# State-space chunks stored by place in a block, gate products held back during the scan, rotation split into additions and a background rest

## The chip, the cores and the metric

The kernel runs on one core of one Trainium2 chip, in one launch. The metric is the device time of that launch in microseconds (us), as a median of runs. A profile of one execution gives, engine by engine, what each instruction did. The engines are PE (matrix multiply, with its weight loads shown apart as PEld), DVE (vector), ACT (scalar: copies, activations), POOL and SP; here SP issues nearly all DMA transfers, one after the other from one queue.

## The reference, cut to what matters

One decoder layer on 512 tokens of width 2048, in float32:

```python
h = rmsnorm(x, g_mix) * (1 + sc1) + sh1
u, q, k, v = jnp.split(h @ w_in, ...)
y_ssm = s5_mixer(u, ...)                       # diagonal complex state space, then gelu and a gate
y_att = dilated_attention(q, k, v, positions)  # q and k rotated (rope), three dilated branches
y = jnp.concatenate([rmsnorm(y_ssm), rmsnorm(y_att)], axis=-1)
x = x + gt1 * (y @ w_out)
h = rmsnorm(x) * (1 + sc2) + sh2
x = x + gt2 * ((silu(h @ w_gate) * (h @ w_up)) @ w_down)
```

The six vectors sh1, sc1, gt1, sh2, sc2, gt2 are `silu(c) @ w_mod + b_mod`: one vector times a matrix of 2048 by 12288, called gate products below. The mixer's recurrence over tokens is s[t] = a * s[t-1] + b u[t] for 64 groups of 64 complex states. Rotation is t1 * cos - t2 * sin and t2 * cos + t1 * sin on the two halves of a head.

## The kernel before, in words

Each large matrix product is done in three passes (`mm3`, L191 to L193): a float32 weight is split into a rounded part `hi` (ACT, L161) and a rest `lo` (DVE, L165), and so is the activation. A product of 512 output rows takes weight pieces of two 128-row blocks; a piece is 24 matmuls on PE (4 row groups, 2 blocks, 3 passes), with three buffers for the split pieces and five for the raw ones that SP loads (L153). Results go to four banks `g` in the accumulator memory (PSUM), and the next product's first matmul into a bank waits until that bank is read.

Beside the products run generators (`start`, `pump`): before each 128-row block of a product, `pump` advances every background generator by its rate. A scheduler then sets the order on each engine, which may put an instruction ahead of one that the code wrote earlier; the order rows below show what it made.

The stage around the change begins with `win3`. Four products of w_in finish q and k (blocks 0, 2, 1, 3 of 512 rows, with 12, 10, 12 and 10 row blocks left to do). After each, `rope(b)` rotates the four results: `r0` loads the partial sum stored earlier (L900, from `part`), adds the bank to it (L901, this frees the bank) and has ACT copy the two halves crosswise (L903); `r1` does two products and a sum on DVE (L908 to L910) and stores (L912). Before the change `r0` of one result and `r1` of the result before it alternate, all at the end of the product, in a pool `rt` of four tiles.

Beside them runs `s5_main` at rate 1. The 512 tokens are 64 chunks j of T = 8 tokens; u is stored and loaded by chunk. PE makes the chunks' inputs (L790), ACT copies them to the state tile X (L797), [128 partitions, real and imaginary, 32 groups, 1 + 64 chunks]. The scan on DVE sees the 64 chunks as 8 blocks b of 8 places i, j = 8 b + i. For i = 1 to 7 four instructions of 512 elements handle all 8 blocks at once (L814, L815, L817, L818); so neighbouring elements of X lie 8 floats, 32 bytes, apart. Then seven steps over the blocks' ends (L823 to L825, 128 and 64 elements), then eight pairs that add each block's start to its inner places (L835, L837, 784 elements). Then, for eight parts of eight groups, the output phase: ACT copies states to `sst` (L845), SP loads tables `mt` (L852) and `qt` (L861), PE multiplies (L866, L867), ACT applies gelu (L874), PE transposes (L883), ACT writes the result back in token order (L886). The first `mt` shares its buffer with the scan's last temporary, so it loads only when the scan is over.

The generator `mod_blocks(GT1)` runs at rate 0.28 from `win3`: each step loads 512 KB of w_mod (L305, three buffers `mraw`) and multiplies on DVE (L314). After `win4` (products with w_glu, which need the whole output of the state space) `mod_blocks(SC2, SH2)` runs as well, beside the attention; both take the next piece from one list of 160, the last of which the feed-forward stage needs.

Of the kernel before, what the change touches and what calls it, by code (L numbers as in the profile page):

```python
# [10 lines left out]
F32 = mybir.dt.float32  # L11
# [3 lines left out]
ALU = mybir.AluOpType  # L15

P = 128
S = 512
# [9 lines left out]
EPS = 1e-6  # L28
T = 8
NJ = S // T  # L30
SCALE = 128 ** -0.5

V_BMOD, V_GMIX, V_GFFN, V_GFIN, V_BGLU, V_GSSM, V_GATT, V_C = 0, 96, 112, 128, 144, 152, 160, 168
# [12 lines left out]
def hybrid_block(ctx: ExitStack, tc: tile.TileContext, xT, crow, vecs, pos, kc, km, w_mod, w_in, s5a, s5bc,  # L46
# [279 lines left out]
    def mod_blocks(*bases, after=None):  # L326
        for b in bases:
# [6 lines left out]
            if b == SC2:  # L334
                modulate(gs2, SC2, V_GFFN)

    def sumsq(acc, x, first):
# [250 lines left out]
    def u_store(pss):  # L588

        for m, ps in enumerate(pss):  # L590
            t = st()
            ACT.copy(t.rearrange("p (s j) -> p s j", s=T), ps.rearrange("p (j s) -> p s j", s=T))
            SP.dma_start(ud[m * P:(m + 1) * P], t)

    gemm(wiv, UC, 0, range(KT), act_h, u_store, w=2 * S)
# [176 lines left out]
    def s5_main():  # L772
        with tc.tile_pool(name="s5m", bufs=1, side="right", reuse_waits="tile") as sp, \
                tc.tile_pool(name="s5n", bufs=2, side="right", reuse_waits="tile") as sq:
            X = sp.tile([P, 2, NG // 2, NJ + 1], F32, name="s5X")
            DVE.memset(X[:, :, :, 0:1], 0.0)
            st_ = {}
            Ug = U[0]


            def u2(c):
                st_[c] = dict(pm=[vg[:, (2 * c + i) % 8].rearrange("p (g x) -> p g x", g=4) for i in range(2)])
                for i, pm in enumerate(st_[c]["pm"]):
                    SP.dma_start(pm, Pd[2 * c + i].rearrange("p (g x) -> p g x", g=4))

            def u3(c):
                d = st_[c]
                d["pi"] = mps()
                for i in range(8):
                    PE.matmul(d["pi"][:, i * NJ:(i + 1) * NJ], d["pm"][i // 4][:, i % 4], Ug[:, 8 * c + i], start=True,  # L790
                              stop=True)

            def u4(c):
                pv = st_.pop(c)["pi"].rearrange("p (g h j) -> p g h j", h=2, j=NJ)
                for h in range(2):
                    for r in range(2):
                        ACT.copy(X[64 * h:64 * h + 64, r, 4 * c:4 * c + 4, 1:], pv[64 * r:64 * r + 64, :, h])  # L797

            yield from pipe(range(8), u2, skip, u3, u4)
            yield  # L800

            NB = NJ // 8
            Xv = X[:, :, :, 1:].rearrange("p r g (b i) -> p r g b i", i=8)

            def bb(a):
                return a.unsqueeze(3).to_broadcast([P, 2, NP, NB])

            def rgb(tag):
                return sq.tile([P, 4, P], F32, tag="tA", name=nm(tag)).rearrange(
                    "p a b -> p (a b)").rearrange("p (r g b) -> p r g b", r=2, g=NP)  # L810

            for i in range(1, 8):
                t0, t1 = rgb("t0"), rgb("t1")
                tt(t0, Xv[:, :, :, :, i - 1], bb(A8[:, 0]), op=ALU.mult)  # L814
                tt(t1, Xv[:, :, :, :, i - 1], bb(A8[:, 1]), op=ALU.mult)  # L815
                yield
                tt(Xv[:, :, :, :, i], Xv[:, :, :, :, i], t0, op=ALU.add)  # L817
                tt(Xv[:, :, :, :, i], Xv[:, :, :, :, i], t1[:, ::-1], op=ALU.add)  # L818
                yield
            tmp = sp.tile([P, 2, 2, NP], F32, name="s5t")  # L820
            for b in range(1, NB):
                xn = Xv[:, :, :, b, 7]
                tt(tmp, Xv[:, :, :, b - 1, 7].unsqueeze(1).to_broadcast([P, 2, 2, NP]), A64, op=ALU.mult)  # L823
                tt(xn, xn, tmp[:, 0], op=ALU.add)
                tt(xn, xn, tmp[:, 1, ::-1], op=ALU.add)  # L825
                if b % 3 == 0:
                    yield
            for h in range(2):
                pr = slice(16 * h, 16 * h + 16)
                for o, r, p_, op in ((0, 0, 0, ALU.add), (0, 1, 1, ALU.subtract), (1, 1, 0, ALU.add),  # L830
                                     (1, 0, 1, ALU.add)):
                    t = sp.tile([P, T, P], F32, tag="tB", name=nm("tc")).rearrange("p a b -> p (a b)")
                    t = t[:, :16 * 49].rearrange("p (g b i) -> p g b i", g=16, b=7)
                    xo = Xv[:, o, pr, 1:, 0:7]
                    tt(t, Xv[:, r, pr, 0:7, 7].unsqueeze(3).to_broadcast([P, 16, 7, 7]),  # L835
                       PW[:, p_, pr, 0:7].unsqueeze(2).to_broadcast([P, 16, 7, 7]), op=ALU.mult)
                    tt(xo, xo, t, op=op)  # L837
                    yield

            def y0(c):  # L840
                prs = slice(4 * c, 4 * c + 4)
                sst = sq.tile([P, 8, NJ], F32, tag="tC", name=nm("sst")).rearrange("p (a b) j -> p a b j", b=2)
                for h in range(2):
                    for r in range(2):
                        ACT.copy(sst[64 * r:64 * r + 64, :, h], X[64 * h:64 * h + 64, r, prs, 0:NJ])  # L845
                st_[c] = dict(sst=sst)

            def y0b(c):
                mt = vg[:, (0, 4, 6)[i]:][:, :2].rearrange("p a (b x) -> p (a b) x", x=P) if (
                    i := (0, 1, 2, 0, 1, 2, 0, 2)[c]) else sp.tile([P, T, P], F32, tag="tB", name=nm("mt"))  # L850
                kc0 = Kd[:, c * P:(c + 1) * P]
                SP.dma_start(mt, bass.AP(tensor=kc0.tensor, offset=kc0.offset,  # L852
                                         ap=[[WS, P], [GC * WS, T], [1, P]]))
                st_[c]["mt"] = mt

            def y1(c):
                d = st_[c]
                d["ps"] = []
                for hh_ in range(2):
                    qt = sq.tile([P, 4, P], F32, tag="tA", name=nm("qt"))  # L860
                    SP.dma_start(qt, Qd[2 * c + hh_].rearrange("p (g x) -> p g x", g=4))  # L861
                    ps = mps()
                    for i in range(4):
                        g = 4 * hh_ + i
                        o = ps[0:NJ, i * P:(i + 1) * P]
                        PE.matmul(o, Ug[:, 8 * c + g], d["mt"][:, :, g * GC:(g + 1) * GC], start=True, stop=False)  # L866
                        PE.matmul(o, d["sst"][:, g // 2, g % 2], qt[:, i], start=False, stop=True)  # L867
                    d["ps"].append(ps)

            def y2(c):  # L870
                d = st_[c]
                d["yv"] = yv = sp.tile([NJ, T, P], F32, tag="ug", name=nm("yv"))
                for hh_, ps in enumerate(d["ps"]):
                    ACT.activation(  # L874
                        yv[:, :, hh_ * 64:hh_ * 64 + 64].rearrange("p t (g c) -> p g t c", g=4),
                        ps[0:NJ].rearrange("p (g t c) -> p g t c", g=4, t=T), AF.Gelu_apprx_tanh)

            def y3(c):
                d = st_[c]
                d["pt"] = mps()  # L880
                for t_ in range(T):
                    sl = T - 1 - t_
                    PE.transpose(d["pt"][:, sl * NJ:(sl + 1) * NJ], d["yv"][:, t_], ident[:NJ, :NJ])  # L883

            def y4(c):
                ACT.copy(vg[:, c].rearrange("p (j s) -> p s j", s=T),  # L886
                         st_.pop(c)["pt"].rearrange("p (s j) -> p s j", s=T))

            yield from pipe(range(8), y0, y0b, y1, y2, y3, y4)

# [2 lines left out]
    def rope(b):  # L893

        def f(pss):
            ts = {}

            def r0(m):
                ts[m] = pt, sw = [rst.tile([P, S], F32, tag="rt", name=nm("rt")) for _ in range(2)]
                SP.dma_start(pt, part[4 * b + m])  # L900
                tt(pt, pss[m], pt, op=ALU.add)  # L901
                for h in (0, 64):
                    ACT.copy(sw[64 - h:128 - h], pt[h:h + 64])  # L903
# [666 lines left out]
```

## Time and profile before

| what | before |
|---|---|
| runs, us | 2193.1, 2188.76, 2193.03 |
| median, us | 2193.03 |
| the profiled execution's own time, us | 2189.05 |
| its span, us | 2187.2 |
| mean granted TensorE clock | 0.984 |
| PE / DVE / ACT busy, share of the span | 96% / 69% / 39% |

The span is what the profile shows between the first and the last instruction; the own time is what was measured for that same execution. A share of busy time is a mean over stages with different limits, so a stage has to be looked at in its own stretch of time. Around this change the landmarks are, in us from the span's start: first scan instruction 352.6, last one 464.2, first output matmul of the state space 470.2, last output copy 519.4.

### The profile page before, as it was taken

The page shows a single profiled execution, that of the slowest core. Times are in us where ns is not written, and L with a number is a line of the kernel's source. Part 1 is how long each engine was busy: PE and PEld are TensorE (multiplying, and loading weights), DVE is VectorE, ACT ScalarE, POOL GpSimd, SP SyncE. Part 2 cuts the span into 40 slices and gives each one's busy share as a digit, 9 for nine tenths or more (in the row PEclk, how much of TensorE's full clock was granted, in tenths as well). Part 3 has the DMA queues.
Part 4 walks back from the last instruction along what each step waited for, and adds up shares of the span by engine and source line. Part 5 has one row for each costly group of instructions (what it writes and reads, how often), then busy time and mean ns, then how long its engine had stood idle before and what let it go on. Part 6 is the DMA issues. An engine that isn't in the chain of part 4 may idle for free.

```text
span 2187.2 us, 32392 instructions
## 1 busy us (share of the span) xinstructions
PE 2109.8 (96%) x12800; PEld 1874.8 (86%) x12800; DVE 1516.8 (69%) x2216; ACT 849.6 (39%) x1209; POOL 2.0 (0%) x7
## 2 busy tenths in 40 slices
PE   6999999889999999999999999999999999999996
PEld 4778787767787778999999999999999888888885
DVE  7896886986888776687887888878887543242224
ACT  3432343257753253444444444444444111121111
POOL 0000000000000000000000000000000000000000
PEclk9999988999999999999999999999999999999998
DMA  9999785768887633343343333434435999655552
GB/s 344 339 357 174 215 248 197 238 210 296 299 284 249 219 114 97 130 144 123 135 138 132 128 135 131 143 123 136 138 132 217 323 320 327 204 195 194 193 173 77
DMA packets 212047, 435.92 MB, mean 199 GB/s; under 512 B 50676, under 2 KB 87924, under 8 KB 211896
## 3 DMA queue, kind: packets, MB, share of 16 engines
q1 hardware_dynamic: 211656, 433.13, 59.8%
q8 instruction: 101, 1.65, 0.3%
q0 software_dynamic: 240, 0.72, 0.1%
q14 instruction: 50, 0.41, 0.1%
HBM read 380.38 MB, written 53.41 MB: 198 GB/s over the span
## 4 chain that ended last, share of the span: by engine, by line
PE 73%; DVE 8%; DMA 3%; issue 1%; ACT 0%; DVEq 0%; SPq 0%; ACTq 0%
PE g L191 11%; PE g L193 11%; PE g L192 11%; PE y L1436 5%; PE y L1437 5%; PE y L1438 5%; PE z L1437 3%; PE x L1437 3%; PE x L1436 3%; PE z L1436 3%; PE x L1438 3%; PE z L1438 3%; DMA mraw<-in_w_mod 3%; DVE mraw L314 1%; DVE lo L165 1%
## 5 line engine op out<-in xcount | busy, mean ns | idle before, releaser
L165 DVE TENSOR_TENSOR lo<-raw,hi 128x1024 fp32r<-128x1024 f32 x192 | 234.2, 1221 | 323.8 <-ACT hi L161 323.7
L161 ACT CAST hi<-raw 128x1024 fp32r<-128x1024 f32 x192 | 201.6, 1052 | 557.4 <-PE g L192 356.3
L1167 ACT CAST hi<-raw 128x1024 fp32r<-128x1024 f32 x176 | 185.1, 1052 | 292.5 <-PE x L1437 125.4
L314 DVE SCALAR_TENSOR_TENSOR mraw<-mraw,cb 128x1024 f32<-128x1024 f32 x192 | 232.1, 1219 | 75.8 <-DMA mraw<-in_w_mod 75.6
L1169 DVE TENSOR_TENSOR lo<-raw,hi 128x1024 fp32r<-128x1024 f32 x176 | 215.1, 1223 | 90.2 <-ACT hi L1167 90.1
L191 PE MATMUL g<-f,hi 128*128 128x512 f32 x704 | 273.9, 389 | 0.0
L192 PE MATMUL g<-f,hi 128*128 128x512 f32 x704 | 273.9, 389 | 0.0
L193 PE MATMUL g<-f,lo 128*128 128x512 f32 x704 | 273.9, 389 | 0.0
L1167 ACT CAST hi<-s 128x1024 fp32r<-128x1024 f32 x120 | 126.3, 1053 | 165.0 <-PE y L1437 82.8
L1436 PE MATMUL y<-t,hi 128*128 128x256 f32 x640 | 179.8, 281 | 0.0
L1437 PE MATMUL y<-t,hi 128*128 128x256 f32 x640 | 179.8, 281 | 0.0
L1438 PE MATMUL y<-t,lo 128*128 128x256 f32 x640 | 179.8, 281 | 0.0
L1437 PE MATMUL x<-b,hi 128*128 128x256 f32 x640 | 179.8, 281 | 0.0
L1436 PE MATMUL x<-b,hi 128*128 128x256 f32 x640 | 179.8, 281 | 0.0
L1438 PE MATMUL x<-b,lo 128*128 128x256 f32 x640 | 179.8, 281 | 0.0
L1169 DVE TENSOR_TENSOR lo<-s,hi 128x1024 fp32r<-128x1024 f32 x120 | 146.5, 1221 | 16.3 <-ACT hi L1167 15.7
L193 PEld LDWEIGHTS g<-f,lo 128*128 128x128 f32 x704 | 132.1, 188 | 27.5
L191 PEld LDWEIGHTS g<-f,hi 128*128 128x128 f32 x704 | 132.1, 188 | 27.4
L192 PEld LDWEIGHTS g<-f,hi 128*128 128x128 f32 x704 | 132.1, 188 | 27.3
L191 PE MATMUL g<-hB,hi 128*128 128x512 f32 x288 | 115.6, 403 | 12.8 <-DVE rt L901 12.8
L1436 PEld LDWEIGHTS x<-b,hi 128*128 128x128 f32 x640 | 120.6, 188 | 0.0
L1437 PEld LDWEIGHTS x<-b,hi 128*128 128x128 f32 x640 | 120.6, 188 | 0.0
(321 smaller groups left out, 4935.4 us busy)
## 6 DMA issues: line engine op xcount, KB each, us to landing
mraw<-in_w_mod SPq DMA_DIRECT2D x192, 512.0 KB, 6.0
raw<-in_w_down SPq DMA_DIRECT2D x88, 512.0 KB, 3.9
f<-fd SPq DMA_DIRECT2D x88, 512.0 KB, 4.2
raw<-in_w_gate SPq DMA_DIRECT2D x80, 512.0 KB, 3.3
raw<-in_w_up SPq DMA_DIRECT2D x80, 512.0 KB, 3.8
raw<-in_w_in SPq DMA_DIRECT2D x64, 512.0 KB, 5.2
fd<-fo SPq DMA_DIRECT2D x40, 512.0 KB, 4.5
raw<-in_w_out SPq DMA_DIRECT2D x32, 512.0 KB, 5.4
```

The lines of the kernel that those rows point to most:

```text
L161: ACT.copy(hi, p["raw"])
L165: tt(p["hl"][1], p["raw"], p["hl"][0].bitcast(F32), op=ALU.subtract)
L191: PE.matmul(ps, lhs[0], rhs[0], start=first, stop=False)
L192: PE.matmul(ps, lhs[0], rhs[1], start=False, stop=False)
L193: PE.matmul(ps, lhs[1], rhs[0], start=False, stop=last)
L314: stt(raw, raw, 1.0, cb[:, h * (D // 2):(h + 1) * (D // 2)], op0=ALU.mult, op1=ALU.mult, accum_out=macc[:, m, h:h + 1])
L1167: ACT.copy(hi, raw)
L1169: tt(lo, raw, hi.bitcast(F32), op=ALU.subtract)
L1436: PE.matmul(o, hi[:, sl], bh[:, k], start=f, stop=False, skip_group_check=True)
L1437: PE.matmul(o, hi[:, sl], bo[:, k], start=False, stop=False, skip_group_check=True)
L1438: PE.matmul(o, lo[:, sl], bh[:, k], start=False, stop=l, skip_group_check=True)
```

## The change

1. Chunks are stored by place in a block, then by block: j' = 8 i + b. `u_store` writes u in that order (ACT now reads the bank with a step of 64 floats along b), X gets 8 columns ahead of the 64 instead of one, and the scan's eight elements of one place lie side by side. One DVE copy is new: it puts the seven block ends into columns 1 to 7, so that columns 0 to 63 are again "the state before each chunk". The last output copy (L886 before, L898 after) writes tokens in order from the new chunk order, with a step of 64 floats where it was 8.
2. `away` wraps `mod_blocks(GT1)`: the generator takes no step while 'scan' is in `made`, which is set from the scan's first to its last step; its rate becomes 0.45.
3. `rope`: the four `r0` come first, in one go; the four `r1` become a generator at rate 1. The partial sum now lies in the staging pool (`st`, five tiles, shared with other copies), and only the crosswise copy in `rt`.

```diff
-            X = sp.tile([P, 2, NG // 2, NJ + 1], F32, name="s5X")
+            NB = NJ // NI
+            X = sp.tile([P, 2, NG // 2, NB + NJ], F32, name="s5X")
...
-            Xv = X[:, :, :, 1:].rearrange("p r g (b i) -> p r g b i", i=8)
+            made.add('scan')
+            Xv = X[:, :, :, NB:].rearrange("p r g (i b) -> p r g i b", i=NI)
...
-                tt(t0, Xv[:, :, :, :, i - 1], bb(A8[:, 0]), op=ALU.mult)
+                tt(t0, Xv[:, :, :, i - 1], bb(A8[:, 0]), op=ALU.mult)
...
+            DVE.tensor_copy(X[:, :, :, 1:NB], Xv[:, :, :, 7, 0:7])
...
+            made.remove('scan')
...
-            ACT.copy(t.rearrange("p (s j) -> p s j", s=T), ps.rearrange("p (j s) -> p s j", s=T))
+            ACT.copy(t.rearrange("p (s i b) -> p s i b", s=T, i=NI), ps.rearrange("p (b i s) -> p s i b", s=T, i=NI))
...
-                ts[m] = pt, sw = [rst.tile([P, S], F32, tag="rt", name=nm("rt")) for _ in range(2)]
+                ts[m] = pt, sw = st(), rst.tile([P, S], F32, tag="rt", name=nm("rt"))
...
-            for _ in pipe(range(4), r0, r1):
-                pass
+            def rest():
+                for m in range(4):
+                    r1(m)
+                    yield
+            for m in range(4):
+                r0(m)
+            hh.append(start(rest(), 1))
...
-        hg.append(start(mod_blocks(GT1), 0.28))
+        hg.append(start(away(mod_blocks(GT1), 'scan'), 0.45))
```

The first rotation on DVE (the end of the first of the four products) stood so before; `g_2725` to `g_2728` are the four banks, `lo_` the next weight pieces:

```order
L901 TENSOR_TENSOR rt_3028<-g_2725,rt_3028 128x512
L165 TENSOR_TENSOR lo_3069<-raw_2757,hi_3068 128x1024
L818 TENSOR_TENSOR s5X<-s5X,t_3115 128x64x8
L908 TENSOR_TENSOR rt_3028<-rt_3028,cosT 128x512
L909 TENSOR_TENSOR rt_3029<-rt_3029,sinT 128x512
L814 TENSOR_TENSOR t_3153<-s5X,A_248 128x512
L910 TENSOR_TENSOR rt_3028<-rt_3028,rt_3029 128x512
L901 TENSOR_TENSOR rt_3038<-g_2726,rt_3038 128x512
```

And so now, where L913 is the addition and L920 to L922 the rest:

```order
L913 TENSOR_TENSOR st_3034<-g_2725,st_3034 128x512
L828 TENSOR_TENSOR s5X<-s5X,t_3065 128x64x8
L315 SCALAR_TENSOR_TENSOR mraw_2958,macc<-mraw_2958,cb 128x1024
L913 TENSOR_TENSOR st_3040<-g_2726,st_3040 128x512
L920 TENSOR_TENSOR st_3034<-st_3034,cosT 128x512
L913 TENSOR_TENSOR st_3046<-g_2727,st_3046 128x512
L913 TENSOR_TENSOR st_3052<-g_2728,st_3052 128x512
```

Between the first two additions stood six instructions, now two; the fourth followed 21 instructions after the first, now six. In later products the four additions stand in one run, or one scan step apart.

The steps over the block ends (L823 to L825 before, L833 to L835 now) stand on DVE like this before:

```order
L823 TENSOR_TENSOR s5t<-s5X,A_249 128x128
L165 TENSOR_TENSOR lo_3472<-raw_3226,hi_3471 128x1024
L824 TENSOR_TENSOR s5X<-s5X,s5t 128x64
L314 SCALAR_TENSOR_TENSOR mraw_3599,macc<-mraw_3599,cb 128x1024
L825 TENSOR_TENSOR s5X<-s5X,s5t 128x64
L314 SCALAR_TENSOR_TENSOR mraw_3737,macc<-mraw_3737,cb 128x1024
```

and like this now:

```order
L833 TENSOR_TENSOR s5t<-s5X,A_249 128x128
L315 SCALAR_TENSOR_TENSOR mraw_3912,macc<-mraw_3912,cb 128x1024
L834 TENSOR_TENSOR s5X<-s5X,s5t 128x64
L315 SCALAR_TENSOR_TENSOR mraw_4156,macc<-mraw_4156,cb 128x1024
L835 TENSOR_TENSOR s5X<-s5X,s5t 128x64
L315 SCALAR_TENSOR_TENSOR mraw_4167,macc<-mraw_4167,cb 128x1024
```

So gate products still stand inside the scan, since the scheduler moves them up to where it sees DVE idle. From the scan's first to its last instruction DVE has 15 weight splits, 13 gate products and 48 rotation instructions before, and 14, 9 and 45 now, beside the scan's own 28, 21 and 16 (and the new copy).

On PE the last inputs of the chunks (L790 before, L800 now) stand before the scan; before, both of the last two parts in one go:

```order
L193 MATMUL g_2728<-hB_100,lo_2813 128x512
L790 MATMUL m_2945<-s5U,vg 128x64 x8
L790 MATMUL m_2958<-s5U,vg 128x64 x8
L191 MATMUL g_2725<-hB_100,hi_2872 128x512
L192 MATMUL g_2725<-hB_101,hi_2872 128x512
```

and now the last of them in two halves, inside the next weight piece (`lo_2876`):

```order
L192 MATMUL g_2727<-hB_100,hi_2875 128x512
L800 MATMUL m_2964<-s5U,vg 128x64 x4
L193 MATMUL g_2727<-hB_101,hi_2875 128x512
L194 MATMUL g_2727<-hB_100,lo_2876 128x512
L800 MATMUL m_2964<-s5U,vg 128x64 x4
L192 MATMUL g_2727<-hB_100,hi_2875 128x512
```

Counted from the first L790, 39 of the product's matmuls stand ahead of the last L790 before, and 54 ahead of the last L800 now. Ahead of the first output matmul of the state space (L866 before, L878 now) stand 462 of 471 such matmuls before, and 453 now. Up to the first of the attention's score readings (L1047) DVE has done 94 gate products before and 91 now.

More of the change, by code (lines that the diff above doesn't have):

```diff
@@ L30 @@
 NJ = S // T
+NI = 8
 SCALE = 128 ** -0.5
@@ L335, in mod_blocks, with away @@
                 modulate(gs2, SC2, V_GFFN)
+    def away(gen, mark):
+        for _ in gen:
+            yield
+            while mark in made:
+                yield
     def sumsq(acc, x, first):
@@ L796, in u4 @@
                     for r in range(2):
-                        ACT.copy(X[64 * h:64 * h + 64, r, 4 * c:4 * c + 4, 1:], pv[64 * r:64 * r + 64, :, h])
+                        ACT.copy(X[64 * h:64 * h + 64, r, 4 * c:4 * c + 4, NB:], pv[64 * r:64 * r + 64, :, h])
             yield from pipe(range(8), u2, skip, u3, u4)
             yield
-            NB = NJ // 8
-            Xv = X[:, :, :, 1:].rearrange("p r g (b i) -> p r g b i", i=8)
+            made.add('scan')
+            Xv = X[:, :, :, NB:].rearrange("p r g (i b) -> p r g i b", i=NI)
             def bb(a):
@@ L810, in rgb @@
                     "p a b -> p (a b)").rearrange("p (r g b) -> p r g b", r=2, g=NP)
-            for i in range(1, 8):
+            for i in range(1, NI):
                 t0, t1 = rgb("t0"), rgb("t1")
-                tt(t0, Xv[:, :, :, :, i - 1], bb(A8[:, 0]), op=ALU.mult)
-                tt(t1, Xv[:, :, :, :, i - 1], bb(A8[:, 1]), op=ALU.mult)
+                tt(t0, Xv[:, :, :, i - 1], bb(A8[:, 0]), op=ALU.mult)
+                tt(t1, Xv[:, :, :, i - 1], bb(A8[:, 1]), op=ALU.mult)
                 yield
-                tt(Xv[:, :, :, :, i], Xv[:, :, :, :, i], t0, op=ALU.add)
-                tt(Xv[:, :, :, :, i], Xv[:, :, :, :, i], t1[:, ::-1], op=ALU.add)
+                tt(Xv[:, :, :, i], Xv[:, :, :, i], t0, op=ALU.add)
+                tt(Xv[:, :, :, i], Xv[:, :, :, i], t1[:, ::-1], op=ALU.add)
                 yield
@@ L821, in s5_main @@
             for b in range(1, NB):
-                xn = Xv[:, :, :, b, 7]
-                tt(tmp, Xv[:, :, :, b - 1, 7].unsqueeze(1).to_broadcast([P, 2, 2, NP]), A64, op=ALU.mult)
+                xn = Xv[:, :, :, 7, b]
+                tt(tmp, Xv[:, :, :, 7, b - 1].unsqueeze(1).to_broadcast([P, 2, 2, NP]), A64, op=ALU.mult)
                 tt(xn, xn, tmp[:, 0], op=ALU.add)
@@ L832, in s5_main @@
                     t = sp.tile([P, T, P], F32, tag="tB", name=nm("tc")).rearrange("p a b -> p (a b)")
[L833 to L836, printed above, removed]
+                    t = t[:, :16 * 49].rearrange("p (g i b) -> p g i b", g=16, b=7)
+                    xo = Xv[:, o, pr, 0:7, 1:]
+                    tt(t, Xv[:, r, pr, 7, 0:7].unsqueeze(2).to_broadcast([P, 16, 7, 7]),
+                       PW[:, p_, pr, 0:7].unsqueeze(3).to_broadcast([P, 16, 7, 7]), op=ALU.mult)
                     tt(xo, xo, t, op=op)
                     yield
+            made.remove('scan')
             def y0(c):
@@ L885, in y4 @@
             def y4(c):
-                ACT.copy(vg[:, c].rearrange("p (j s) -> p s j", s=T),
-                         st_.pop(c)["pt"].rearrange("p (s j) -> p s j", s=T))
+                ACT.copy(vg[:, c].rearrange("p (b i s) -> p s i b", s=T, i=NI),
+                         st_.pop(c)["pt"].rearrange("p (s i b) -> p s i b", s=T, i=NI))
             yield from pipe(range(8), y0, y0b, y1, y2, y3, y4)
@@ L912, in r1 @@
                 SP.dma_start((qd if i < 8 else kd)[(i % 8) * P:(i % 8 + 1) * P], pt)
-            for _ in pipe(range(4), r0, r1):
-                pass
+            def rest():
+                for m in range(4):
+                    r1(m)
+                    yield
+            for m in range(4):
+                r0(m)
+            hh.append(start(rest(), 1))
         return f
```

## Prediction

> **What bounds the kernel now.** I read the page first, then the table by stretches of time around the scan, then waits, groups and timeline of that stretch. The page's busy rows and its chain of waits say that PE sets the time almost everywhere:
>
> ```profile
> PE   6999999889999999999999999999999999999996
> DVE  7896886986888776687887888878887543242224
> ...
> PE 73%; DVE 8%; DMA 3%; issue 1%; ACT 0%; DVEq 0%; SPq 0%; ACTq 0%
> ```
>
> Each digit is 54.7 us. DVE holds 8% of the chain, and it is the only engine beside PE that holds much. Where it does, the table by stretches shows (busy us of PE, PEld, DVE, ACT, POOL; then granted clock, DMA share, GB/s):
>
> ```profile
> 352.00:464.00 112.00, 98.34 (x401) 77.23 (x400) 109.75 (x154) 35.55 (x50) 0.00 (x0) 0.95 0.65 216
> 464.00:518.00 54.00, 49.59 (x366) 40.48 (x364) 29.25 (x45) 37.49 (x65) 0.56 (x1) 1.00 0.88 283
> 518.00:562.00 44.00, 43.90 (x204) 35.80 (x205) 35.83 (x75) 32.57 (x53) 0.00 (x0) 1.00 0.85 279
> ```
>
> The first row is the scan with three of the four rotations: DVE works 109.75 of 112 us, PE idles 112 - 98.3 = 13.7 us and runs at 0.95 of its clock (5% of 112 = 5.6 us). In the next two rows DVE has 24.8 and 8.2 us free and PE is full again. PE's waits in this stretch are for DVE:
>
> ```profile
> PE g L191 <- DVE rt L901: 12.8, 8, 3.0
> PE g L193 <- DVE lo L165: 0.9, 2, 0.6
> ```
>
> 12.8 us in eight waits go to the addition that frees a bank, which stands in DVE's queue behind scan steps, gate products and the other rotations' work. One such wait on PE's timeline, and the matmul after it, beside the one before it:
>
> ```profile
> 364.43 0.39 PE L191 MATMUL g<-hB,hi 128*128 128x512 f32 x1
> 367.79 0.79 PE L191 MATMUL g<-hB,hi 128*128 128x512 f32 x1 [2.97 <-DVE rt L901]
> 368.38 0.63 PE L192 MATMUL g<-hB,hi 128*128 128x512 f32 x1
> 368.81 0.63 PE L193 MATMUL g<-hB,lo 128*128 128x512 f32 x1
> ```
>
> After 2.97 us of idling the matmuls start 0.43 us apart; undisturbed ones do so every 0.227 us:
>
> ```profile
> 463.49 0.39 PE L191 MATMUL g<-hB,hi 128*128 128x512 f32 x1
> 463.71 0.39 PE L192 MATMUL g<-hB,hi 128*128 128x512 f32 x1
> ...
> 468.25 0.39 PE L193 MATMUL g<-hB,lo 128*128 128x512 f32 x1
> 470.22 0.41 PE L866 MATMUL m<-mt,s5U 128*64 128x128 f32 x2 [1.59 <-DMA mt<-Kd]
> ```
>
> (21 steps from 463.49 to 468.25.) The last line is the scan's end as PE sees it, 1.59 us more of waiting. So the scan's end sets when the output phase starts, and PE can win at most 13.7 + 5.6 + 1.6 = 20.9 us here.
>
> **The change part by part.** DVE's work from the scan's first to its last instruction, by groups:
>
> ```profile
> L165 DVE TENSOR_TENSOR lo<-raw,hi 128x1024 fp32r<-128x1024 f32 x16 | 19.3, 1209 | 0.0
> L314 DVE SCALAR_TENSOR_TENSOR mraw<-mraw,cb 128x1024 f32<-128x1024 f32 x13 | 15.7, 1208 | 1.4 <-DMA mraw<-in_w_mod 1.4
> L818 DVE TENSOR_TENSOR s5X<-s5X,t 128x512 f32<-128x512 f32 x7 | 8.2, 1177 | 0.0
> L901 DVE TENSOR_TENSOR rt<-g,rt 128x512 f32<-128x512 f32 x12 | 8.1, 678 | 0.0
> ...
> L817 DVE TENSOR_TENSOR s5X<-s5X,t 128x512 f32<-128x512 f32 x7 | 8.1, 1155 | 0.0
> L814 DVE TENSOR_TENSOR t<-s5X,A 128x512 f32<-128x512 f32 x7 | 7.9, 1135 | 1.9 <-ACT s5X L797 1.8
> L815 DVE TENSOR_TENSOR t<-s5X,A 128x512 f32<-128x512 f32 x7 | 7.8, 1109 | 0.0
> L837 DVE TENSOR_TENSOR s5X<-s5X,tc 128x784 f32<-128x784 f32 x8 | 7.7, 966 | 0.0
> ...
> L824 DVE TENSOR_TENSOR s5X<-s5X,s5t 128x64 f32<-128x64 f32 x7 | 1.9, 267 | 0.0
> ```
>
> It runs from 352.62 to the end of the last L837, with 1.4 us of idling after its start:
>
> ```profile
> 352.62 1.18 DVE L814 TENSOR_TENSOR t<-s5X,A 128x512 f32<-128x512 f32 x1 [1.83 <-ACT s5X L797]
> ...
> 463.19 0.97 DVE L837 TENSOR_TENSOR s5X<-s5X,tc 128x784 f32<-128x784 f32 x1
> 464.08 1.22 DVE L165 TENSOR_TENSOR lo<-raw,hi 128x1024 fp32r<-128x1024 f32 x1
> ```
>
> Scan steps. The 28 steps of 512 elements take 8.2 + 8.1 + 7.9 + 7.8 = 32.0 us, 1144 ns each, with elements 32 bytes apart. L901 does 512 contiguous ones in 678. Runs of eight at a row pitch of 288 bytes are not in the trace. The nearest row is L837: runs of seven, 784 elements in 966 ns, so 288 ns for 272 elements more than L901, 1.06 ns each, as fast as contiguous (678 less a start of some 140 over 512). I take 678: 28 x 0.466 = 13.0 us less; the ends are 0 (nothing gained from runs) and the same 13.0. L823 to L825 and L835 to L837 keep their prices: single far-apart elements and runs of seven before and after. The new copy of 448 elements lies between L824 (267 ns) and L901 (678); I take 0.45 us.
>
> Gate products. The order leaves 9 of 13 in the scan: 4 x 1.21 = 4.8 us less. They return elsewhere: DVE's 24.8 us free from 464 to 518 hide them. Up to the attention's first score three are still owed; without cover they cost 3.7 us.
>
> Rotation and splits. 45 for 48 rotation instructions, 14 for 15 splits: 3 x 0.678 + 1.2 = 3.2 us less, done after the scan under the same cover. The sum for DVE: 13.0 + 4.8 + 3.2 - 0.45 = 20.5 us.
>
> Given back on PE. The last chunk inputs now stand behind 54 instead of 39 matmuls: the scan starts 15 x 0.227 = 3.4 us later, so its end comes 17.1 us earlier. The first `mt` transfer follows it as before. Behind the first output matmul stand nine more matmuls of the products (462 - 453): 2.0 us. From there to the end of the w_glu products PE is full in both, so **15.1 us** remain. Against PE's cap of 20.9 that leaves some 6 us of waiting in the scan, mostly for weight splits that still stand between scan and rotation near its end.
>
> Banks and staging. With the four additions at most a few instructions apart, a bank is freed about 0.7 us after the one before, where PE needs one every six matmuls, 1.36 us; this is where the 12.8 us go. What is late next is the partial sums: a staging tile is free for the next sum only when its rotated result is stored, and SP's queue waits for that with weight loads behind it. A load lands in this time (minimum, median, maximum), over both uses of the old tiles:
>
> ```profile
> DMA to landing us min/median/max: 2.0/3.1/6.1
> ```
>
> In the order, between the first product's last rotation and the next additions stand 12 scan steps, three gate products and two splits, 12 x 0.68 + 5 x 1.21 = 14 us; store and load take two of these times, 6.2 us. So I cost it at nothing; without that cover see the third rival.
>
> Copies on ACT. `u_store`'s eight bank reads change their step, and so do the eight output writes:
>
> ```profile
> L592 ACT COPY st<-g x8: 580/588/590, 183.6 to 190.1; 128x512 f32<-128x512 f32 x8
> L538 ACT COPY st<-g x24: 573/587/613, 60.8 to 294.5; 128x512 f32<-128x512 f32 x24
> L886 ACT COPY vg<-m x8: 1067/1088/1197, 478.1 to 519.4; 128x512 f32<-128x512 f32 x8
> ```
>
> A bank read 32 bytes apart (L592) costs what a contiguous one does (L538); at 256 bytes I take the same 588 ns, the upper end being L886's 1088: 4.0 us, hidden since 1.09 is below PE's 1.36 per bank, 4.0 us without that. [...] The scattered writes (L886) stay at 1088; the ends, 587 and the longest, 1197, make -4.0 to +0.9 us on an ACT with 16.5 us free in that stretch.
>
> The sum: 2189.05 - 15.1 = 2174 against the profiled execution's own time, and 2193.03 - 15.1 = 2178 against the median of the runs shown, which lies 4 us higher; I predict 2176, from the middle of the two, 2191; the rivals are reckoned from there too. About 0.2%, 4.4 us, is what a measurement of this kernel can tell from no change: its runs spread by that.
>
> The clock: after a 2.97 us wait the trace shows half speed. [...]
>
> **The rivals.** First, the layout gains nothing: runs of eight cost 1144 as before. Then DVE saves 7.5 us, the later start and the nine matmuls take 5.4, and 2 us remain: 2189, no change. For it: no row has this pitch. Against: L837. Chance 0.08.
>
> Second, the gate stream takes part of it back. From 562 to 800 it runs beside the attention on the same DVE queue:
>
> ```profile
> L314 DVE SCALAR_TENSOR_TENSOR mraw<-mraw,cb x56: 1204/1221/1228, 561.4 to 741.0; 128x1024 f32<-128x1024 f32 x56
>   DMA mraw<-in_w_mod: 18.7, 16
> ...
> 797.23 1.40 DVE L1219 SCALAR_TENSOR_TENSOR st<-x,gs,m 128x512 f32<-128x512 f32 x2
> ```
>
> 56 products in 180 us are 3.2 us each; three more owed make 9.6 us if the stream sets the pace there: 15.1 - 9.6 = 5.5 us of gain, 2185. For it: 18.7 us of DVE waiting for w_mod. Against: the stream ends at 741 and is first read for the feed-forward stage at 797 (L1219), so 9.6 us later would still be in time. Chance 0.14.
>
> Third, slower: the staging pool. If rotations run so late that stores and loads are not hidden, each of three handovers waits for three loads in a row, 9.3 us at the median of 3.1, 28 us in all: +28 - 15 = 13 over, 2204. It decides once a rotation ends less than 6.2 us before PE needs the next sum. For it: SP's queue blocks as a whole. Against: the 14 us above. Chance 0.10.
>
> Fourth, PE reaches its cap of 20.9 us and the output phase's waits shrink too: 2168. Chance 0.06.
>
> **How the numbers follow.** The forecast has 0.62, with its own range 2168 to 2183 (gains of 8 to 23 from 2191). Faster by over 0.2% are the forecast, the fourth rival and 0.12 of the second: 0.80. Within 0.2% are the first and the rest of the second: 0.10. Slower has 0.10. The range for 8 in 10 takes in the second rival and the runs' spread: 2165 to 2188.
>
> **What would show it.** In the profile after: scan steps near 680 ns (the step that carries most; at 1144 the forecast falls); scan end 17 us earlier, at about 447; PE's wait for L913 down from 12.8 to below 5 us; the stretch from the first output matmul to the end of w_glu's products as long as before plus 2 us; DVE's wait for w_mod from 562 on not longer by more than 4 us. The prediction is wrong if PE waits for L913 behind part loads, or if the lead of the scan's end has shrunk by the time the attention ends.

## The result, and the profile after

| | before | after |
|---|---|---|
| median, us (lowest to highest, 7 runs each) | 2193.1 (2188.76 to 2193.8) | 2180.1 (2173.05 to 2185.12) |
| ratio to before, 95% interval | | 0.9939 (0.9921 to 0.9958) |
| the profiled execution's own time, us | 2189.05 | 2180.85 |
| its span, us | 2187.2 | 2179.1 |

The kernel is 13.0 us faster at the median (9 to 17 by the interval). The page of the profile hardly shows it. Its chain of waits reads, after the change:

```profile
PE 72%; DVE 8%; DMA 4%; issue 1%; ACT 0%; SPq 0%; DVEq 0%; ACTq 0%
```

DVE still holds 8% of the chain. The difference has to be looked for in its own stretch. The table by stretches of the kernel after shows the scan, the output phase, and the rest of the w_glu products (columns as in the prediction):

```profile
358.73:449.98 91.25, 85.65 (x373) 69.63 (x372) 90.16 (x144) 34.99 (x48) 0.00 (x0) 0.99 0.65 217
449.98:507.17 57.19, 53.70 (x377) 43.20 (x376) 31.55 (x48) 37.30 (x65) 0.56 (x1) 0.96 0.87 285
507.17:552.30 45.13, 45.13 (x205) 36.66 (x206) 37.90 (x80) 34.28 (x53) 0.00 (x0) 1.00 0.78 268
```

The scan lasts 91.25 us where it lasted 111.5. DVE is still busy in all but about 1 us of it. PE idles 91.25 - 85.65 = 5.6 us instead of 13.7, and its clock is 0.99 instead of 0.95. What shortened it stands in the instructions on the state tile:

```profile
L846 DVE TENSOR_TENSOR tc<-s5X,PW x8: 962/966/968, 426.1 to 447.0; 128x784 f32<-128x784 f32 x8
L824 DVE TENSOR_TENSOR t<-s5X,A x7: 673/680/693, 358.7 to 400.7; 128x512 f32<-128x512 f32 x7
L827 DVE TENSOR_TENSOR s5X<-s5X,t x7: 675/679/686, 359.9 to 403.8; 128x512 f32<-128x512 f32 x7
L833 DVE TENSOR_TENSOR s5t<-s5X,A x7: 378/389/402, 407.9 to 425.3; 128x128 f32<-128x128 f32 x7
...
L838 DVE COPY s5X<-s5X x1: 380/380/380, 425.6 to 425.6; 128x448 f32<-128x448 f32 x1
```

A scan step costs 680 ns (L824, L827) where it cost 1144; the instructions with far-apart elements or runs of seven (L833, L846) kept their prices (389 ns for 382, 966 for 966); the new copy (L838) takes 0.38 us. So 512 float32 elements 32 bytes apart took 1144 ns, and in runs of eight they take 680, no more than contiguous ones did (678, L901 before).

PE's waits for DVE from 340 to 470 are now:

```profile
PE g L194 <- DVE lo L166: 3.3, 1, 3.3
PE g L192 <- DVE st L913: 2.3, 2, 1.6
```

The 12.8 us for additions have become 2.3. The longest wait is now for a weight split, near the end of the scan, as PE's timeline shows it:

```profile
449.15 0.80 PE L194 MATMUL g<-hB,lo 128*128 128x512 f32 x1 [3.28 <-DVE lo L166]
```

The scan itself now stands on DVE from

```profile
358.73 0.69 DVE L824 TENSOR_TENSOR t<-s5X,A 128x512 f32<-128x512 f32 x1 [4.75 <-ACT s5X L807]
...
449.01 0.97 DVE L848 TENSOR_TENSOR s5X<-s5X,tc 128x784 f32<-128x784 f32 x1
```

It starts 6.1 us later than before and ends 14.2 us earlier. The first output matmul comes at 457.07 (470.22 before), the end of the w_glu products at 552.3 (562.3), the end of the span 8.1 us earlier: a lead of 14 us at the scan's end is 10 at the end of w_glu and 8 at the end of this one execution, while the medians differ by 13. What belongs to the change in this, and what to the single execution, the experiments had to tell.

### The profile page after: what moved, and what is told of

It is laid out like the page before. It is cut to its first block, busy times and chain, and to the rows that moved or that the text cites. A ratio compares the mean times of both kernels' runs of the same rounds, so it can differ in the third digit from the quotient of the medians.

```text
span 2179.1 us, 32377 instructions
## 1 busy us (share of the span) xinstructions
PE 2111.1 (97%) x12800; PEld 1877.5 (86%) x12800; DVE 1504.6 (69%) x2217; ACT 849.9 (39%) x1209; POOL 2.0 (0%) x7
## 4 chain that ended last, share of the span: by engine, by line
PE 72%; DVE 8%; DMA 4%; issue 1%; ACT 0%; SPq 0%; DVEq 0%; ACTq 0%
PE g L194 11%; PE g L192 11%; PE g L193 11%; PE y L1454 5%; PE y L1455 5%; PE y L1456 5%; PE x L1454 3%; PE z L1454 3%; PE x L1455 3%; PE z L1455 3%; PE z L1456 3%; PE x L1456 3%; DMA mraw<-in_w_mod 3%; DVE mraw L315 1%; DVE lo L166 1%; PE m L800 1%
## 5 line engine op out<-in xcount | busy, mean ns | idle before, releaser
L166 DVE TENSOR_TENSOR lo<-raw,hi 128x1024 fp32r<-128x1024 f32 x192 | 234.3, 1221 | 320.6 <-ACT hi L162 320.3
L315 DVE SCALAR_TENSOR_TENSOR mraw<-mraw,cb 128x1024 f32<-128x1024 f32 x192 | 232.3, 1219 | 82.3 <-DMA mraw<-in_w_mod 82.0
L1454 PEld LDWEIGHTS y<-t,hi 128*128 128x128 f32 x640 | 120.6, 188 | 0.4 <-issue 0.4
```

What stands on the lines that cost most here:

```text
L166: tt(p["hl"][1], p["raw"], p["hl"][0].bitcast(F32), op=ALU.subtract)
L315: stt(raw, raw, 1.0, cb[:, h * (D // 2):(h + 1) * (D // 2)], op0=ALU.mult, op1=ALU.mult, accum_out=macc[:, m, h:h + 1])
L1454: PE.matmul(o, hi[:, sl], bh[:, k], start=f, stop=False, skip_group_check=True)
```

## The experiments

A ratio is the time against the kernel before, run beside it; gains in us are worked out from it with the 2192.5 us of before; intervals are 95%. e1 to e12 name the runs.

**A book for PE.** Each version does the same matrix work, so a difference in time must be a difference in what PE loses. In a stretch, that is the elapsed time less PE's busy time, and the part of the clock that was not granted. For the scan before it is 13.7 + 5.6 = 19.3 us, for the scan after 5.6 + 1% of 91.25 = 6.5. The clock has two digits, so each figure is good to half a microsecond.

| version | PE loses in the scan, us | less than before | measured gain, us | ratio (interval) |
|---|---|---|---|---|
| before, second profile (e9) | 13.2 + 5.6 = 18.8 | 0.5 | -0.9 | 1.0004 (0.9993 to 1.0014) |
| part 2 alone (e10) | 17.3 + 5.6 = 22.9 | -3.6 | -3.9 | 1.0018 (1.0007 to 1.0029) |
| part 3 alone (e2) | 12.3 + 3.1 = 15.4 | 3.9 | -0.7 | 1.0003 (0.9994 to 1.0012) |
| part 1 alone (e1) | 8.0 + 2.0 = 10.0 | 9.3 | 10.7 | 0.9951 (0.9938 to 0.9964) |
| parts 1 and 2 (e4) | 9.8 + 2.0 = 11.8 | 7.5 | 5.7 | 0.9974 (0.9964 to 0.9984) |
| parts 1 and 3 (e3) | 5.3 + 0.9 = 6.2 | 13.1 | 16.0 | 0.9927 (0.9915 to 0.9938) |
| the same again (e11) | 5.3 + 0.0 = 5.3 | 14.0 | 12.7 | 0.9942 (0.9925 to 0.9958) |
| whole change again (e8) | 5.7 + 0.9 = 6.6 | 12.7 | 11.6 | 0.9947 (0.9934 to 0.9961) |
| whole change, third (e12) | 6.4 + 0.0 = 6.4 | 12.9 | 11.4 | 0.9948 (0.9932 to 0.9964) |
| whole, old rate (e5) | 4.5 + 3.7 = 8.2 | 11.1 | 7.9 | 0.9964 (0.9952 to 0.9976) |
| whole, not held back (e6) | 6.4 + 2.8 = 9.2 | 10.1 | 15.1 | 0.9931 (0.9916 to 0.9946) |
| whole, gates really out (e7) | 1.1 + 0.0 = 1.1 | 18.2 | 12.3 | 0.9944 (0.9929 to 0.9960) |

Seven of the twelve rows agree within 2 us. In e2, e5 and e7 3 to 6 us of what the scan gives are missing at the end; each of them is looked at below. e3 and e6 gained 3 to 5 us more than the scan shows, for which the profiles name no single place.

### One part at a time

Part 1 alone. Against the whole change:

```diff
-        hg.append(start(away(mod_blocks(GT1), 'scan'), 0.45))
+        hg.append(start(mod_blocks(GT1), 0.28))
...
-                ts[m] = pt, sw = st(), rst.tile([P, S], F32, tag="rt", name=nm("rt"))
+                ts[m] = pt, sw = [rst.tile([P, S], F32, tag="rt", name=nm("rt")) for _ in range(2)]
...
-            for m in range(4):
-                r0(m)
-            hh.append(start(rest(), 1))
+            for _ in pipe(range(4), r0, r1):
+                pass
```

> Part 1 alone (chunks by place in a block, the new copy); gate products and rotation as before. In the order nothing else moves: 13 gate products, 15 splits and 48 rotation instructions stand in the scan, 39 matmuls ahead of the last chunk inputs and 462 ahead of the first output matmul, all as before. Theory A (the vector engine's work inside the scan sets when the output phase starts, and the layout is the main term): the scan lasts 28 x 0.466 - 0.45 = 12.5 us less, and the time falls by about 12.5 us (0.57%). Theory B (the gain is banks freed at once, so it sits in the rotation): PE still waits some 12.8 us for the additions, and the time falls by less than 3 us.

Measured: 0.9951, 10.7 us less. The scan's stretch in the table, and then PE's wait for additions (L904 here) in the list of waits:

```profile
350.01:451.65 101.64, 93.62 (x398) 75.08 (x397) 97.82 (x156) 34.97 (x48) 0.00 (x0) 0.98 0.69 235
```

```profile
PE g L192 <- DVE rt L904: 6.5, 4, 2.6
```

The scan is 9.9 us shorter, 2.6 less than reckoned; 2.2 of these are idle time of DVE in it (101.64 - 97.82 = 3.8 us, before 1.6). PE's wait for additions halves although the rotation is untouched. So a good part of those waits was not the order of the rotation but the length of what stood ahead of it. Theory A holds, theory B falls.

Part 3 alone: only the `ts[m]`, `rest` and `r0` lines of the change.

> Part 3 alone (four additions at once, the rest in the background, partial sums in the staging pool); layout and gate products as before. In the order 45 rotation instructions, 13 splits and 10 gate products stand in the scan (48, 15 and 13 before), and 436 instead of 462 matmuls stand ahead of the first output matmul. Theory A: the scan lasts 3 x 0.68 + 2 x 1.2 + 3 x 1.21 = 8.1 us less, and 26 matmuls, 5.9 us, come behind its end, so the time falls by about 2 us. Theory B: PE's waits for the additions go, 12.8 us, and the time falls by about 12 us.

Measured: 1.0003, no difference. The table by stretches for the scan and the output phase, then PE's wait, then the scan steps on DVE:

```profile
353.53:456.85 103.32, 91.05 (x385) 73.55 (x383) 102.22 (x144) 36.25 (x49) 0.00 (x0) 0.97 0.61 208
456.85:517.23 60.38, 53.71 (x371) 43.84 (x372) 30.80 (x47) 36.05 (x65) 0.56 (x1) 0.92 0.82 259
```

```profile
PE g L191 <- DVE st L901: 10.1, 4, 5.9
```

```profile
L818 DVE TENSOR_TENSOR s5X<-s5X,t x7: 1092/1195/1220, 356.9 to 413.1; 128x512 f32<-128x512 f32 x7
```

With the old layout PE still waits 10.1 us for additions, now in four waits, one of 5.9: three banks of four come free quickly, but the first addition stands behind other work all the same. The scan is 8.2 us shorter as reckoned, with 26 matmuls fewer beside it. The 3.9 us that PE gains there go in the output phase, where it idles 6.7 us at a clock of 0.92 (before, from 464.16 to 519.4: 4.5 us at 1.00). So theory A's 2 us are not reached either; theory B falls a second time.

Part 2 alone: `away`, the marks and the rate 0.45 on the kernel before.

> Part 2 alone on the kernel before. In the order 14 gate products (13 before) stand in the scan, 52 matmuls (39 before) ahead of the last chunk inputs, 462 ahead of the first output matmul as before. Theory A: 1.2 us more in the scan and a start 13 x 0.227 = 3.0 us later, so some 4 us slower than before (ratio 1.002). Theory C (holding back helps the scan): 2 us or more faster.

Measured: 1.0018, 3.9 us slower, as theory A has it. The stretch of the scan, and PE's wait for additions (L910 here):

```profile
358.84:470.87 112.03, 94.68 (x382) 73.80 (x381) 110.76 (x157) 34.99 (x48) 0.00 (x0) 0.95 0.62 205
```

```profile
PE g L191 <- DVE rt L910: 16.9, 10, 2.6
```

It holds nothing out of the scan (14 gate products for 13) and starts it later: 35.7 us after the first chunk input on PE, which comes at 323.14 here, where before it was 33.2 us (319.45). So fewer matmuls are left to run beside the scan, and PE idles 17.3 us there. The remaining 3.7 us by which 358.84 is late lie ahead of the stage (see the repeats below).

### Two parts at a time

Parts 1 and 3 (part 2 undone by the first two lines of the diff above):

> Parts 1 and 3 together; the gate generator as before (rate 0.28, no holding back). In the order 10 gate products stand in the scan (9 with part 2, 13 before), 40 matmuls ahead of the last chunk inputs (54 with part 2, 39 before), 453 ahead of the first output matmul. Theory A: scan 13.0 + 3.6 + 2.0 + 1.2 - 0.45 = 19.4 us shorter, start as before, 2.0 us of matmuls behind it: about 17 us less than before, 2 us less than the whole change. Theory C (holding back the gate products is what frees the vector engine): at least 4 us less gain than the whole change's 13 us, so a gain of 9 us or less.

Measured: 0.9927, 16.0 us less. Theory A, with 17, is near; theory C falls. Parts 1 and 2:

> Parts 1 and 2 together; the rotation as before. In the order 14 gate products stand in the scan (13 before), 52 matmuls ahead of the last chunk inputs (39 before), 462 ahead of the first output matmul. Theory A: scan 12.5 - 1.2 us shorter, its start 13 x 0.227 = 3.0 us later: about 8 us less than before. Theory B: PE still waits for the additions, and the gain is below 3 us. Theory C: a gain of 12 us or more, since the wrapped generator keeps the vector engine free.

Measured: 0.9974 (0.9964 to 0.9984), 5.7 us less: somewhat below theory A's 8, well above theory B's 3, and far from theory C's 12. It is 5.0 us worse than part 1 alone, where 4.2 were reckoned for part 2.

So part 3, worth nothing with the old layout, is worth several microseconds with the new one: with it the whole change's three ratios are 0.9939, 0.9947 and 0.9948, without it 0.9974.

### What in part 2 costs

Two versions take part 2 apart, beside the other two parts. First, holding back at the old rate:

```diff
-        hg.append(start(away(mod_blocks(GT1), 'scan'), 0.45))
+        hg.append(start(away(mod_blocks(GT1), 'scan'), 0.28))
```

> The whole change, but the held-back gate generator keeps its old rate of 0.28. In the order 10 gate products, 13 splits and 44 rotation instructions stand in the scan, 40 matmuls (54 in the whole change) ahead of the last chunk inputs, 439 ahead of the first output matmul. Theory A1 (part 2 costs time because its rate of 0.45 brings more work ahead of the last chunk inputs): the start of the scan is early again, near 353; 14 matmuls, 3.2 us, are won there, and 14 more stand behind the scan; the time is within 2 us of the version without part 2 (15.5 us less than before). Theory A2 (holding back itself costs): the time stays at the whole change's 13 us less than before, or above.

Then the new rate without holding back:

```diff
-        hg.append(start(away(mod_blocks(GT1), 'scan'), 0.45))
+        hg.append(start(mod_blocks(GT1), 0.45))
```

> The whole change without the holding back, but with the rate of 0.45. In the order 11 gate products, 14 splits and 47 rotation instructions stand in the scan, 54 matmuls ahead of the last chunk inputs, 455 ahead of the first output matmul. Theory A1 (the rate costs): the scan starts some 3.2 us later than without part 2 and has 1.2 + 1.4 us more in it: 4 to 6 us slower than the version without part 2, so about 10 us less than before. Theory A2 (holding back costs, the rate does not): 15.5 us less than before.

Measured: 0.9964 (0.9952 to 0.9976) and 0.9931 (0.9916 to 0.9946), 7.9 and 15.1 us less than before. Theory A1 is wrong as to the time: both times are those of theory A2, by which holding back costs and the rate doesn't. A1 is right as to the start, if one counts from the first chunk input on PE. The inputs in e3 (neither), in e6 (the rate) and in e5 (holding back) begin and end at:

```profile
L793 PE MATMUL m<-s5U,vg x128: 217/292/421, 319.5 to 350.8; 128*128 128x64 f32 x128
```

```profile
L800 PE MATMUL m<-s5U,vg x128: 217/292/422, 319.5 to 354.1; 128*128 128x64 f32 x128
```

```profile
L800 PE MATMUL m<-s5U,vg x128: 217/292/422, 322.2 to 353.8; 128*128 128x64 f32 x128
```

They last 31.3, 34.6 and 31.6 us: 14 matmuls, 3.2 us, more with the rate of 0.45. The scan starts 33.2, 36.4 and 33.4 us after the first of them. (Counted from the span's start e5's scan starts at 355.60, not near 353 as A1 had it, because its first input is late; see the repeats below.) But a late start costs only what PE then lacks beside the scan, and e6 as a whole measures no different from e3.

Part of e5's loss lies further on. From its scan's end to the first matmul of w_out it takes 108.6 us, e6 101.7; 3.6 of the 6.9 us are the 16 matmuls more (455 - 439) that stand behind its scan. From the end of its w_glu products to the second half of w_out (554 to 696) PE waits for the softmax:

```profile
PE a L1083 <- ACT pt L1088: 6.6, 3, 4.1
```

Before the longest of these waits, which ends at 566.69, DVE and then ACT do:

```profile
559.39 1.23 DVE L315 SCALAR_TENSOR_TENSOR mraw<-mraw,cb 128x1024 f32<-128x1024 f32 x1 [2.74 <-DMA mraw<-in_w_mod]
...
562.36 1.29 DVE L994 TENSOR_TENSOR vg<-vg,st 128x512 f32<-128x512 f32 x2
```

```profile
563.08 1.33 ACT L996 ACTIVATE ys<-vg,vec 128x512 fp32r<-128x512 f32 x2 [2.97 <-DVE vg L994]
564.32 2.17 ACT L358 ACTIVATE st<-vg 128x512 f32<-128x512 f32 x4
566.40 0.24 ACT L1088 COPY pt<-a 128x128 f32<-128x128 f32 x1
```

A gate product waits 2.74 us for its w_mod load at the head of DVE's queue. Behind it, after one more gate product, stand the products of `vg` (L994). ACT waits for these, and the copy `pt` that PE needs stands behind them in ACT's queue. In the whole change the two waits for w_mod around this place are 0.15 and 1.44 us, and PE's waits for `pt` sum to 2.4 (2.6 and 4.0 in its two other profiles). But they sum to 5.2 in the kernel before and to 5.3 in e6. So this wait explains little more than 1 of the 7 us between e5 and e6, and what else holding back costs there stays open: there is one profile of each. Nor does one run tell whether the held-back stream brings the wait about, or only the order that this version happened to get.

### The gate products really out of the scan

The order rows showed that `away` doesn't do what it says. Here the steps after the scan are tied behind its last instruction, and the rate is 0.28:

```diff
-                with tc.issue_after(after.ins) if after is not None else nullcontext():
+                a = after or (last[0] if last and b == GT1 else None)
+                with tc.issue_after(a.ins) if a is not None else nullcontext():
...
-                    tt(xo, xo, t, op=op)
+                    z = tt(xo, xo, t, op=op)
                     yield
+            last.append(z)
```

> The whole change with rate 0.28, and the gate products that follow the scan in the program ordered behind its last instruction, so that they do stay out of it. In the order 1 gate product, 13 splits and 39 rotation instructions stand in the scan (10, 14 and 45 without part 2), 40 matmuls ahead of the last chunk inputs, and 407 instead of 453 ahead of the first output matmul. Theory A: the scan is 9 x 1.21 + 1.2 + 6 x 0.68 = 16.2 us shorter than without part 2, 46 matmuls, 10.4 us, come behind it: some 6 us less than without part 2, about 21 us less than before. Theory D (PE has little left to win in the scan, and the gate products held back are missing time behind it): no gain over the version without part 2, or up to 5 us lost.

Measured: 0.9944 (0.9929 to 0.9960), 12.3 us less than before: no gain over the version without part 2, as theory D has it. The scan and the output phase in the table by stretches, and PE's longest wait behind the scan:

```profile
353.88:433.87 79.99, 78.92 (x348) 64.76 (x347) 78.64 (x121) 32.88 (x46) 0.00 (x0) 1.00 0.55 179
434.00:501.00 67.00, 60.98 (x409) 50.57 (x407) 37.88 (x59) 38.83 (x67) 0.56 (x1) 0.95 0.82 270
```

```profile
PE m L882 <- DMA mt<-Kd: 3.9, 1, 3.9
```

The scan does what theory A says: 80 us, PE busy in 78.9 of them at the full clock, a gain of 18 us in the book. Of that, 6 us go again. In the output phase PE idles 6.0 us at a clock of 0.95 (4.5 us at 1.00 before), 3.9 of it for the first `mt` table. Then PE waits 4.1 us for `pt` as in e5, with a gate product on DVE and ACT's wait for `vg` ahead of it:

```profile
554.63 1.23 DVE L315 SCALAR_TENSOR_TENSOR mraw<-mraw,cb 128x1024 f32<-128x1024 f32 x1 [3.08 <-DMA mraw<-in_w_mod]
```

```profile
558.68 1.33 ACT L1000 ACTIVATE ys<-vg,vec 128x512 fp32r<-128x512 f32 x2 [3.85 <-DVE vg L998]
```

Over 550 to 691 PE's waits for `pt` sum to 6.3 us here, against 2.4, 2.6 and 4.0 in the profiles of the whole change and 3.8 in e3.

So PE's cap in the scan can be reached almost wholly, but the next bounds, table loads and gate products that wait for w_mod, stand right behind it. How much of the 6 us each of them takes, one profile doesn't show.

### The same programs again

> The kernel before, as if it were a change. Every theory: ratio 1.000; it shows how far two profiles of one program differ, stage by stage. If PE's waits ahead of the scan, in the attention and behind it differ by 2 to 4 us from the first profile of before, differences of that size there prove nothing of a change.

> The changed kernel once more, beside the others. Every theory: about 13 us less than before (0.61%); the point is a second profile of it. If the scan again starts near 359, this belongs to the change; theory A expects 352.6 + 3.4 = 356, and the rest of the first profile's delay to come from work ahead of the changed stage that differs from run to run.

> Parts 1 and 3 once more, on one chip with the whole change. The first time they gave 0.9927 and the two runs of the whole change 0.9939 and 0.9947. If part 2 costs time also beside the other parts (theory A: 2 us), the ratio is again about 0.993, 2 to 4 us less than the whole change's; if that was chance, the two agree within 1 us.

> The whole change a third time, to be set beside the version without part 2: 0.994 to 0.995 if part 2 costs time, the same as that version if not.

Measured: 1.0004, 0.9947, 0.9942 and 0.9948. The two profiles of before have spans of 2187.2 and 2194.2 us. Their scans last 111.5 and 111.2 us, those of the three profiles of the whole change 91.2, 91.4 and 92.1: the scan repeats within a microsecond, and the 7 us lie elsewhere. One place is the first 100 us, which the change doesn't touch, here in the first and in the second profile of the whole change:

```profile
0.00:100.00 100.00, 77.49 (x284) 59.87 (x285) 77.12 (x164) 40.20 (x64) 0.20 (x4) 0.95 0.92 337
```

```profile
0.00:100.00 100.00, 77.29 (x290) 59.55 (x291) 78.58 (x166) 40.55 (x65) 0.20 (x4) 0.97 0.93 342
```

At a clock of 0.95 the first has six matmuls fewer behind it by then. The third has 0.95 too. Over all fourteen profiles, the five with 0.95 in this stretch have their first chunk input at 321.2 us or later, the nine with 0.97 or 0.98 at 320.6 or earlier, and one and the same program is on both sides (e8 and e12; e3 and e11). So this lateness belongs to the execution, not to the change.

What does belong to the change shows when one counts from the first chunk input: 1306 or 1307 matmul records stand ahead of it in every profile. In us:

| | first chunk input | scan starts after | scan ends after |
|---|---|---|---|
| before, two profiles | 319.45, 320.19 | 33.2, 33.2 | 144.7, 144.4 |
| whole change, three profiles | 322.63, 320.41, 321.86 | 36.1, 36.6, 36.4 | 127.4, 127.9, 128.5 |

So about 3 of the 6.1 us by which the scan started late are the change's, and the scan's end is 16 to 17 us earlier by this count.

Part 2's price beside the other parts stays open: 0.9927 and 0.9942 without it, 0.9939 to 0.9948 with it, about 2 us, and on one chip (e11, e12) the intervals overlap. The two largest gains are those of versions that do not hold the gate products back (e3, 16.0 us; e6, 15.1), but e3 run again (e11) gained 12.7, no more than the whole change.

## Why the prediction was right, and where its sizes were off

The forecast of 2176 is 4 us below the measured 2180.1: half of that is the gain (13.0 for 15.1), half the base of 2191, where the kernel before measured 2193.1. The mechanism held: DVE's work in the scan sets when the output phase starts, and the layout is the largest part of what shortens it (e1, alone, 10.7 us).

**Scan steps** (the term that carried most): 678 ns forecast, 680 measured, 13.0 us. The start of some 140 ns in it was the author's estimate; operations on two float32 tiles with 512 elements in 680 ns (L910 before) and with 1024 in 1219 (L1265) leave 141 at none. The first rival, that runs of eight gain nothing, falls. The kept prices held (L833, L846), the new copy was 0.38 us for 0.45.

**The sum for DVE**: 20.5 us forecast; the scan's length fell by 20.3 in the first pair of profiles and by 19.9 in the second.

**Given back ahead of the scan**: 3.4 us forecast. Counted from the first chunk input the scan starts 2.9 to 3.4 us later in the three profiles. Its end was forecast 17.1 us earlier; by the same count it is 15.9 to 17.4. Counted from the span's start it is 14.2 in the first pair of profiles and 16.3 in the second (464.63 against 448.35), and the third profile of the whole change ends its scan at 450.38; the difference is the late first input. The step is right. From the scan's end to the first output matmul it took 6.1 and 7.5 us before, 7.1, 7.3 and 6.5 after: the `mt` transfer follows as before.

**Given back behind the scan**: the nine matmuls were 2.0 us, and this term was too small. From the first output matmul to the end of the w_glu products it took 92.1 us (470.22 to 562.3) and 92.9 in the two profiles of before, and 95.2 (457.07 to 552.3), 95.5 and 98.2 in the three of the whole change: 2.3 to 6.2 longer. The forecast called PE full from there on in both; it isn't, as the forecast's own row (49.59 of 54 us) shows: PE still waits for the `qt` tables of the output phase, 2.8 and 3.1 us in the two profiles of before, 3.0, 3.7 and 3.1 in the three of the whole change. This stretch is where most of the 1.7 to 3.7 us between the 15.1 forecast and the 11.4 to 13.4 measured lies, as far as the profiles show it; the interval of the first comparison, 9 to 17 us, still contains 15.1.

**Its own sign of being wrong** has come: the lead of the scan's end did shrink. In the first pair of profiles it is 14.2 us at the scan's end, 10.0 at the end of the w_glu products and 10.7 at the last product of the softmax (687.3 before, 676.6 after). The forecast itself gives back 2.0 of this behind the scan; the rest is the term above.

**What remains of PE's waits**: 6 us forecast, mostly for splits; 3.3 for a split and 2.3 for additions.

**Banks**: the forecast said that putting the additions together is where the 12.8 us go. The layout alone takes 6.3 of them away, the rotation alone 2.7, both together 10.5 (2.3 left). Each part's share depends on the other.

**Copies on ACT** with the new steps, both at the value taken:

```profile
L600 ACT COPY st<-g x8: 577/588/590, 185.4 to 191.9; 128x512 f32<-128x512 f32 x8
...
L898 ACT COPY vg<-m x8: 1056/1080/1143, 469.0 to 507.2; 128x512 f32<-128x512 f32 x8
```

Bank reads at a step of 256 bytes still take 588 ns (588 at 32 bytes, 587 for contiguous ones before), so the row gave the price: for ACT's reads no slowdown shows here. Scattered writes stay at 1080 (1088 before).

**The second rival**, the gate stream beside the attention, did not set the pace in the whole change:

```profile
L315 DVE SCALAR_TENSOR_TENSOR mraw<-mraw,cb x58: 1199/1220/1227, 551.0 to 741.9; 128x1024 f32<-128x1024 f32 x58
...
  DMA mraw<-in_w_mod: 16.2, 19
```

58 products, done at 741.9 (741.0 before), 16.2 us of waiting (18.7); in the other two profiles of the whole change 18.9 and 22.2, the latter done at 749.1. Its mechanism is real all the same: in e5 and e7 one product that waits for its load holds up ACT's copy `pt`, and with it PE, for 4.1 us.

**The third rival**, the staging pool: no addition waits for a partial sum any more (4.9 us before). SP does wait for rotated results before it stores them, 26.6 us in eight waits (29.9 in nine before). The profile puts one wait of a weight split on ACT down to such a load:

```profile
380.86 1.06 ACT L162 CAST hi<-raw 128x1024 fp32r<-128x1024 f32 x1 [4.34 <-DMA st<-part]
```

PE has no wait at that place, so it costs nothing here. **The fourth rival**'s cap was reached in the scan by e7, and did not shorten the whole.

**What the forecast missed** is that part 2 is a loss by itself (3.9 us) and beside part 1 (5.0); beside both other parts its price stays open. It had both halves in hand, the 15 matmuls and the 9 gate products, and credited the four that left the scan to the whole. By the order of e3 three of the four leave with the rotation; holding back removes one.

## What to carry to other kernels

Where one engine is full at every stage, write a change as what that engine loses, stretch by stretch (elapsed less busy, and the clock), for every part of the change alone and in pairs: here parts that share DVE's queue did not add up (gains of 10.7 us for part 1 and -0.7 for part 3 alone, 16.0 and 12.7 together), and one cost (part 2, 3.9 us alone). Lay the elements that one instruction handles side by side first: here that took a scan step from 1144 to 680 ns, and PE's wait for the additions queued behind from 12.8 to 6.5 us (e1). When a stage has been emptied, look at the next handover, and at any instruction there that waits for a load at the head of its engine's queue (a gate product for 2.74 us in e5 and 3.08 in e7).

## What the runs showed of the hardware that was not expected

Matmuls at about half pace, 0.43 us apart where undisturbed ones are 0.227, stand also behind waits shorter than the 2.97 us of the prediction, and do not begin at a fixed point. In the profile of before, after 2.54 us they are there from the second matmul on (the granted clock from 401.4 to 404.8 is 0.54; from 372 to 373.8, with undisturbed ones, 1.00):

```profile
401.40 0.60 PE L191 MATMUL g<-hB,hi 128*128 128x512 f32 x1 [2.54 <-DVE rt L901]
401.79 0.63 PE L192 MATMUL g<-hB,hi 128*128 128x512 f32 x1
402.22 0.63 PE L193 MATMUL g<-hB,lo 128*128 128x512 f32 x1
```

and after 2.59 us only 1.1 us later:

```profile
438.24 0.50 PE L191 MATMUL g<-hB,hi 128*128 128x512 f32 x1 [2.59 <-DVE rt L901]
...
439.04 0.48 PE L191 MATMUL g<-hB,hi 128*128 128x512 f32 x1
439.32 0.63 PE L192 MATMUL g<-hB,hi 128*128 128x512 f32 x1
```

The length of the wait alone does not decide. In e10 the matmuls are 0.43 us apart 1.4 us after the end of a wait of 1.77 us, and in the third profile of the whole change (e12) they start 0.34 and 0.23 us apart after one of 3.25. What else decides, these profiles do not show.

```profile
461.28 0.50 PE L191 MATMUL g<-hB,hi 128*128 128x512 f32 x1 [1.77 <-DVE rt L910]
...
462.68 0.63 PE L193 MATMUL g<-hB,lo 128*128 128x512 f32 x1
463.11 0.63 PE L191 MATMUL g<-hB,hi 128*128 128x512 f32 x1
```

```profile
449.55 0.50 PE L194 MATMUL g<-hB,lo 128*128 128x512 f32 x1 [3.25 <-DVE lo L166]
449.89 0.40 PE L192 MATMUL g<-hB,hi 128*128 128x512 f32 x1
450.12 0.39 PE L193 MATMUL g<-hB,hi 128*128 128x512 f32 x1
```
